# Lift, weights and fetches of a mixed head pair moved by one to two steps in an attention kernel on one core

## The chip, the cores and the metric

The kernel runs on one core of a Trainium2 chip. The metric is the device time of one execution in microseconds (us); of several runs the median is taken. Engines are named as in the profile: PE (TensorE), PEld (its weight load), DVE (VectorE), ACT (ScalarE), POOL (GpSimd), SP (SyncE, which only issues DMAs). ACT and POOL issue DMAs of their own besides their work.

## What is computed

One layer of a decoder trunk on 2048 tokens of width 1024, in float32: attention beside a pooling branch, a gated MLP with a short convolution, a gated embedding, and norms between them. Only the attention's last step matters here. A head's output is a mixture of branches, weighted by their softmax denominators:

```python
for window, dil in DIL_PATTERNS:                 # ((128, 1), (512, 4), (2048, 16))
    o, m, d = _dilated_branch(q, k, v, slopes, window, dil)   # output, row max, denominator
...
w = d * jnp.exp(m - jnp.max(m, axis=0, keepdims=True))
w = w / jnp.sum(w, axis=0, keepdims=True)
return jnp.sum(w[..., None] * o, axis=0)
```

The kernel computes two parts per head: a "near" one (window 128) and a "far" one (the two dilated patterns together). It keeps for each query the negated maximum and the denominator of both parts, and mixes at the end: `exp(lo - max)` with `lo` the smaller of the two negated maxima, a division by the weighted sum of denominators, and two products with the unnormalised outputs.

## The kernel before

The program has three phases: projection (to about 400 us of the profile), attention (to about 720 us), and the rest (out projection, MLP, gate). The attention phase, `phase_attention` (from L486), goes over 8 heads in 4 pairs. A head has 16 blocks of 128 queries, so there are 128 steps `s`, 32 to a pair. PE, ACT, DVE and POOL run in the order in which the code is written; that order is made by the loop over `s` (L739), which at each step calls a fixed list of stages (`CFG["ord"]`, L44), each for the step `s - lag`. In one step DVE does the near maximum (L577), the far maximum (L583), the low part of a split (L617) and often a sum of two halves (L660); ACT does two exponentials (L589, L593), a cast (L613) and a copy (L659); PE does scores (L561, L562, L572, L573), transposes (L600) and products with the values (L628, L642). `CFG["perm"]` turns the blocks so that the four steps of a group have far widths of 512, 384, 256 and 128.

SP loads the next head's queries, keys and biases (one load per step, in the first 8 steps of a head) and the next pair's values, as buffers come free.

The pairs 0, 1 and 2 are mixed while the next pair is being computed (the last pair is mixed in another way, in `last_near`, `last_far`, `last_weights`). The stage "M" (`mix`, L705) does it, by the number `d` of steps since the pair's end, so d = 0 is the first step of the next pair:

- d = 0: `mix_stats` (L761): PE transposes the pair's maxima and denominators, DVE copies them to `sx` and `sy`.
- d = 1: `mix_stats_store`: ACT issues two stores to DRAM, `std<-sx` (L776) and `stf<-sy` (L777).
- d = 4: `mix_stats_load`: ACT issues two loads in another order of axes, `sn<-std` (L784) and `sf<-stf` (L788). They wait for the stores, and what stands behind them on ACT waits too.
- d = `m[0]`: `mix_lift` (L858): three DVE operations of 128x32 (L862, L865, L866), the first of which reads `sn` and `sf`; then one exponential on ACT (L867, `wts<-ex`).
- d = `m[1]`: `mix_weights` (L870): five small DVE operations (L874 to L879), then POOL issues the store `wd<-wts` (L880).
- d = `m[2] + m[3] * c` for the four chunks c of 512 queries: `mix_fetch` (L885): POOL issues two loads `wb<-wd` (L891), each spread over 64 partitions.
- `m[4]` steps after its fetch: `mix_products` (L896): POOL multiplies and adds (L901, L902, L908, into the buffers m1 and m3).
- `m[5]` steps after its fetch: `mix_store` (L917): POOL splits the result (L913, L914) and issues two stores, `mh<-ah` and `ml<-al` (L924, L925).

```python
if d == CFG["m"][0]:
    mix_lift(nc, g, mx, pairs[pr])
if d == CFG["m"][1]:
    mix_weights(nc, g, mx, pr, pairs[pr])
for c in range(NCH):
    if d == CFG["m"][2] + CFG["m"][3] * c:
        mix_fetch(nc, g, mx, nc.gpsimd, pr, pairs[pr], c)
    if d == CFG["m"][2] + CFG["m"][3] * c + CFG["m"][4]:
        mix_products(nc, g, mx, nc.gpsimd, pairs[pr], c)
```

In the list of stages "M" stands ahead of the step's maxima, so the lift of d = 9 is on DVE between the low part (L617) of one step and the near maximum (L577) of the next. POOL has no other work in this phase. At the end of the phase `last_near` (L794) copies the last pair's statistics on DVE (L806) into buffers, one of which is the buffer m3 that POOL's products of pair 2 read last in L908.

Of the kernel before, what the change touches and what calls it, by code (L numbers as in the profile page):

```python
# [20 lines left out]
S = 2048  # L21
# [19 lines left out]
V_N = V_CB + 2 * NF  # L41


CFG = {"tt": 2, "ee": 2, 'ord': [['B', 0], ['M', 0], ['N', 0], ['S', 1], ['o', 7], ['F', 0], ['h', 2], ['nm', 0], ['p', 7], ['fm', 0], ['l', 2], ['T', 1], ['V', 6], ['W', 6], ['ne', 0], ['fe', 0]], 'perm': [3, 2, 1, 0], 'fp': [[0], [1], [2], [3]], 'np': [[0, -1], [1], [2], [3]], 'm': [9, 10, 13, 4, 6, 7]}  # L44


class Shared:
# [438 lines left out]
def phase_attention(tc, g, mx, near_b, far_b):  # L486
# [5 lines left out]
    with ExitStack() as ctx:  # L492
# [42 lines left out]
        def begin(s):  # L535
# [7 lines left out]
            st = steps[s] = Shared()  # L543
            st.n = n = n - n % 4 + CFG["perm"][n % 4]
            st.t, st.pt, st.e = heads[h], pairs[h // 2], h % 2
# [5 lines left out]
            st.d1, st.d3 = st.pt.st1[:, 1, st.e, n : n + 1], st.pt.st3[:, st.r, 1, st.e, st.i : st.i + 1]  # L551
            st.tt = sb.tile([P, 768], F32, tag="tt", bufs=CFG["tt"], name="tt")
            st.ee = sb.tile([P, 768], F32, tag="ee", bufs=CFG["ee"], name="ee")

# [64 lines left out]
        def near_pv(gi, kbs, first):  # L619
            gr, q0 = groups[gi], 4 * (gi % 4)  # L620
            for kb in kbs:
                if q0 + kb < 0:
                    continue
                m0, m1 = max(0, kb), min(3, kb + 1)
                b0, b1 = 4 * m0 + kb + 1, 4 * m1 + kb + 1
                kt = q0 + kb
                for pt in (gr.h, gr.l):
                    nc.tensor.matmul(  # L628
                        gr.o[:, m0 * P : (m1 + 1) * P],
                        vals[gi // 8, "v1", kt // 4][:, kt % 4, gi // 4 % 2, :],  # L630
                        pt[:, b0 : b1 + 1 : 4, :],
                        start=first,
                        stop=False,
                        skip_group_check=True,
                    )
                    first = False

        def far_pv(gi, kbs, first):
            gr = groups[gi]
            for kb in kbs:  # L640
                for pt in (gr.h, gr.l):
                    nc.tensor.matmul(  # L642
                        gr.o[:, kb * P :],
                        vals[gi // 8, "v3", gi % 4][:, kb, gi // 4 % 2, :],
                        pt[:, 6 * kb + 2 : 18 + kb : 5, :],
                        start=first,
                        stop=False,
                        skip_group_check=True,
                    )
                    first = False  # L650
# [11 lines left out]
        def values(v):  # L662
# [4 lines left out]
            if part < 2:  # L667
                far_pv(gi, CFG["fp"][2 * part], part == 0)
            else:
                near_pv(gi, CFG["np"][2 * part - 4], part == 2)  # L670

        def values_b(v):
            gi, part = v // 4, v % 4
            if part < 2:
                far_pv(gi, CFG["fp"][2 * part + 1], False)
            else:
# [1210 lines left out]
```

## Time and profile before

| what | value |
|---|---|
| median of 3 runs | 2520.25 us (2514.61, 2520.25, 2520.33) |
| the profiled execution | 2522.12 us, its span 2519.8 us |
| mean granted TensorE clock | 0.98 |
| busy: PE, DVE, ACT, POOL | 2407.5, 1588.8, 1108.6, 515.7 us |
| std store issued, pairs 0, 1, 2 | at 475.48, 551.84, 637.59 us |
| sf load issued, pairs 0, 1, 2 | at 484.64, 562.66, 646.01 us |
| L862 started, pairs 0, 1, 2 | at 498.30, 582.36, 665.04 us |

Rows of the timeline give the start, the duration, the engine, line and operation, output and inputs, and in brackets how long the engine had been idle before it and what ended that idle time. Rows of the waits give who waited for whom: total, times, longest. Rows of the chain of waits give the start and length of each piece of the chain that ended last. Rows of the stage table give a stretch, its length, the busy time of PE, PEld, DVE, ACT and POOL (with the number of instructions), the granted clock, the DMA share and GB/s.

### The profile page before, as it was taken

To read this page: it belongs to the slowest core of one execution; us is meant where nothing else is said; L and a number is where in the kernel's file an instruction comes from. 1 tells how busy PE (TensorE), PEld (TensorE's weight loads), DVE (VectorE), ACT (ScalarE), POOL (GpSimd) and SP (SyncE) were. 2 spreads that over 40 slices of the span, in tenths; PEclk is the share of its full clock that TensorE was granted. 3 is DMA by queue.
4 is the path that set the end of the run, shared out by engine and by line. 5 is a ranking of instruction groups with operands and counts; after the bars stand their busy time and mean duration, and the time that the engine had idled before them with its cause. 6 is when DMAs were issued, how large, how long until landed. Compare 5 with 4: busy or idle time off the path is not lost.

```text
span 2519.8 us, 31897 instructions
## 1 busy us (share of the span) xinstructions
PE 2407.5 (96%) x11515; PEld 2022.4 (80%) x11515; DVE 1588.8 (63%) x2416; ACT 1108.6 (44%) x1923; POOL 515.7 (20%) x423
## 2 busy tenths in 40 slices
PE   8999998888779999999999999999999999999998
PEld 7888887777767877888887888888788888887888
DVE  6635427777774467888888666666535374435755
ACT  5423326887751135544446444444323242323322
POOL 3312221053430023333340000000122222221000
PEclk9999999999879999999999999999999999999999
DMA  7534358687646674555556334333546464635332
GB/s 240 174 120 180 142 178 248 166 193 180 164 164 221 223 252 167 167 177 181 175 194 211 122 117 138 121 114 117 191 134 222 149 219 150 208 122 173 124 105 88
DMA packets 209052, 424.08 MB, mean 168 GB/s; under 512 B 42464, under 2 KB 68896, under 8 KB 205824
## 3 DMA queue, kind: packets, MB, share of 16 engines
q1 hardware_dynamic: 170576, 368.41, 46.4%
q0 software_dynamic: 18672, 25.88, 3.1%
q10 hardware_dynamic: 19648, 27.77, 3.1%
q8 instruction: 90, 1.47, 0.2%
q14 instruction: 66, 0.54, 0.1%
HBM read 290.01 MB, written 131.89 MB: 167 GB/s over the span
## 4 chain that ended last, share of the span: by engine, by line
PE 79%; DMA 6%; DVE 6%; issue 3%; ACT 2%; POOL 0%; SPq 0%; ACTq 0%; POOLq 0%; DVEq 0%
PE ua L1315 18%; PE uc L1315 9%; PE dn L90 6%; PE dn L91 6%; PE dn L89 6%; PE ub L1315 4%; PE z L91 4%; PE z L89 4%; PE z L90 4%; PE o L89 2%; PE o L91 2%; PE o L90 2%; PE gp L89 2%; PE gp L91 2%; PE gp L90 2%
## 5 line engine op out<-in xcount | busy, mean ns | idle before, releaser
L89 PE MATMUL dn<-ah,hd 128*128 128x512 f32 x704 | 275.3, 391 | 2.8 <-ACT ah L84 2.8
L90 PE MATMUL dn<-al,hd 128*128 128x512 f32 x704 | 274.9, 391 | 1.7 <-DVE al L85 1.7
L91 PE MATMUL dn<-ah,ld 128*128 128x512 f32 x704 | 274.6, 390 | 0.0
L85 POOL TENSOR_TENSOR ld<-rd,hd 128x1024 fp32r<-128x1024 f32 x42 | 100.9, 2403 | 812.8 <-ACT hd L84 812.8
L84 ACT CAST hd<-rd 128x1024 fp32r<-128x1024 f32 x88 | 92.5, 1052 | 266.3 <-PE dn L90 230.9
L85 DVE TENSOR_TENSOR al<-ra,ah 128x512 fp32r<-128x512 f32 x88 | 116.8, 1330 | 136.0 <-ACT ah L84 136.0
L89 PE MATMUL z<-hnh,wh 128*128 128x512 f32 (+1 forms) x480 | 170.3, 355 | 9.9 <-ACT hnh L252 5.8
L90 PE MATMUL z<-hnl,wh 128*128 128x512 f32 (+1 forms) x480 | 170.0, 354 | 2.7 <-DVE hnl L253 2.6
L91 PE MATMUL z<-hnh,wl 128*128 128x512 f32 (+1 forms) x480 | 169.9, 354 | 2.3 <-POOL wl L85 1.7
L89 PEld LDWEIGHTS dn<-ah,hd 128*128 128x128 f32 x704 | 132.7, 188 | 31.0 <-ACT ah L84 3.2
L90 PEld LDWEIGHTS dn<-al,hd 128*128 128x128 f32 x704 | 132.7, 188 | 29.8 <-DVE al L85 2.2
L91 PEld LDWEIGHTS dn<-ah,ld 128*128 128x128 f32 x704 | 132.7, 189 | 27.4
L85 DVE TENSOR_TENSOR wu<-ru,wu 128x1024 fp32r<-128x1024 f32 x88 | 127.4, 1448 | 0.0
L155 DVE TENSOR_TENSOR acc<-acc,sq 128x512 f32<-128x512 f32 (+1 forms) x125 | 90.2, 722 | 47.6 <-ACT sq L154 34.6
L1315 PE MATMUL uc<-a22h,wu 128*128 128x512 f32 x352 | 115.7, 389 | 1.8 <-DVE uv L1338 1.8
L1315 PE MATMUL ua<-s2h,wu 128*128 128x512 f32 x352 | 115.8, 390 | 1.1 <-ACT ug L1452 1.1
L1315 PE MATMUL uc<-s3h,wu 128*128 128x512 f32 x352 | 116.2, 390 | 0.3 <-ACT s3h L1371 0.3
L1315 PE MATMUL ub<-a12h,wu 128*128 128x512 f32 x352 | 115.9, 390 | 0.3 <-ACT a12h L1371 0.3
L1315 PE MATMUL ua<-s4h,wu 128*128 128x512 f32 x352 | 115.5, 389 | 0.0
L1315 PE MATMUL ua<-s1h,wu 128*128 128x512 f32 x352 | 115.5, 389 | 0.0
L1315 PE MATMUL ua<-a11h,wu 128*128 128x512 f32 x352 | 115.5, 389 | 0.0
L85 DVE TENSOR_TENSOR ld<-rd,hd 128x1024 fp32r<-128x1024 f32 x46 | 56.2, 1223 | 89.1 <-ACT hd L84 89.1
(317 smaller groups left out, 6474.4 us busy)
## 6 DMA issues: line engine op xcount, KB each, us to landing
rd<-in_w_down_dram SPq DMA_DIRECT2D x88, 512.0 KB, 3.6
ru<-in_w_up_dram SPq DMA_DIRECT2D x66, 512.0 KB, 4.1
ra<-act SPq DMA_DIRECT2D x88, 256.0 KB, 3.8
act<-yg SPq DMA_DIRECT2D x43, 512.0 KB, 3.1
wr<-in_w_in_dram SPq DMA_DIRECT2D x64, 256.0 KB, 4.0
nt<-h SPq DMA_DIRECT2D x56, 256.0 KB, 3.9
h<-h SPq DMA_DIRECT2D x56, 256.0 KB, 5.6
td<-t SPq DMA_DIRECT2D x22, 512.0 KB, 2.6
```

The lines of the kernel that those rows point to most:

```text
L84: nc.scalar.copy(hi, src)
L85: (low or nc.gpsimd).tensor_tensor(lo, src, fp(hi), op=ALU.subtract)
L89: nc.tensor.matmul(ps, wh, ah, start=first, stop=False)
L90: nc.tensor.matmul(ps, wh, al, start=False, stop=False)
L91: nc.tensor.matmul(ps, wl, ah, start=False, stop=last)
L155: nc.vector.tensor_tensor(acc[:, :n], acc[:, :n], sq[:, :n], op=ALU.add)
L1315: nc.tensor.matmul(pst, x[:, ksl], y, start=first and k == 0 and n == 0, stop=k == HK - 1 and n == 2, skip_group_check=True)
```

## The change

One line changes, the table `CFG` at L44, in its last entry `m`:

```diff
-'m': [9, 10, 13, 4, 6, 7]
+'m': [11, 12, 14, 4, 5, 6]
```

The lift is at d = 11 instead of 9 and the weights at d = 12 instead of 10. The fetches of the four chunks are at d = 14, 18, 22, 26 instead of 13, 17, 21, 25. The products come 5 steps behind their fetch instead of 6, that is, at 19, 23, 27, 31 in both kernels, and the stores at 20, 24, 28, 32 in both.

The instructions of PE and of SP stand in the same order in both kernels. POOL's do too: only the buffers' numbers differ, since its fetches, products and stores pass no other POOL instruction. On DVE and ACT the lift and the weights change places. This is the difference on DVE at pair 1's lift (the row of L862 is the lift's first operation; rows with ISA are the maxima, each with the row that reads its result; `ptl` is the low part, `s` the sum of halves):

```order
+L577 ISA tt,st_5565<-sn,nb_5117 128x256
+L577 ISA st_5565 128x1
+L583 ISA tt,st_5566<-sf,fb_5118 128x384
+L583 ISA st_5566 128x1
+L617 TENSOR_TENSOR ptl<-tp,pth 128x384
+L577 ISA tt,st_5565<-sn,nb_5117 128x256
+L577 ISA st_5565 128x1
+L660 TENSOR_TENSOR s_5567<-o,ev 64x512
+L583 ISA tt,st_5566<-sf,fb_5118 128x256
+L583 ISA st_5566 128x1
+L617 TENSOR_TENSOR ptl<-tp,pth 128x768
 L862 TENSOR_TENSOR lo<-sn,sf 128x32
```

The DVE work of two steps (far widths 384 and 256) now stands ahead of L862, the first reader of `sf`; in the rows of L577 and L583 `sn` and `sf` are score tiles of the same name in PSUM, not the loaded statistics. On ACT, at the same place, the exponential of the lift (L867) moves in the same way:

```order
 L593 ACTIVATE ee,st_5566<-tt,st_5566 128x512
+L613 CAST pth<-tp 128x384
+L589 ACTIVATE ee,st_5565<-tt,st_5565 128x256
+L593 ACTIVATE ee,st_5566<-tt,st_5566 128x384
+L659 COPY ev<-o 64x512
+L613 CAST pth<-tp 128x768
+L589 ACTIVATE ee,st_5565<-tt,st_5565 128x256
+L593 ACTIVATE ee,st_5566<-tt,st_5566 128x256
 L867 ACTIVATE wts<-ex 128x64
```

Seven ACT operations of the same two steps now stand ahead of L867. The pieces at pairs 0 and 2 are alike.

More of the change, by code (lines that the diff above doesn't have):

```diff
@@ L41 @@
 V_N = V_CB + 2 * NF
-CFG = {"tt": 2, "ee": 2, 'ord': [['B', 0], ['M', 0], ['N', 0], ['S', 1], ['o', 7], ['F', 0], ['h', 2], ['nm', 0], ['p', 7], ['fm', 0], ['l', 2], ['T', 1], ['V', 6], ['W', 6], ['ne', 0], ['fe', 0]], 'perm': [3, 2, 1, 0], 'fp': [[0], [1], [2], [3]], 'np': [[0, -1], [1], [2], [3]], 'm': [9, 10, 13, 4, 6, 7]}
+CFG = {"tt": 2, "ee": 2, 'ord': [['B', 0], ['M', 0], ['N', 0], ['S', 1], ['o', 7], ['F', 0], ['h', 2], ['nm', 0], ['p', 7], ['fm', 0], ['l', 2], ['T', 1], ['V', 6], ['W', 6], ['ne', 0], ['fe', 0]], 'perm': [3, 2, 1, 0], 'fp': [[0], [1], [2], [3]], 'np': [[0, -1], [1], [2], [3]], 'm': [11, 12, 14, 4, 5, 6]}
 class Shared:
```

## The prediction

> **What bounds the kernel now.** I read the page first, then the stage table, the waits, the chain and the timelines of the attention phase.
>
> ```profile
> PE 2407.5 (96%) x11515; PEld 2022.4 (80%) x11515; DVE 1588.8 (63%) x2416; ACT 1108.6 (44%) x1923; POOL 515.7 (20%) x423
> ```
>
> PE bounds the program as a whole. The change touches only the attention phase, and there the picture is another. The waits from 398 to 740 us:
>
> ```profile
> ACT wts L867 <- DVE ex L866: 13.7, 3, 7.2
> DVE lo L862 <- DMA sf<-stf: 12.9, 2, 6.9
> PE sn L572 <- DVE st L577: 13.6, 3, 6.4
> ```
>
> Twice DVE stands at the lift's first operation because the statistics `sf` haven't landed; ACT then stands at the lift's exponential, and PE runs out of work, since its next scores need the maximum (L577) queued behind the lift. The chain that ended last goes through these two loads:
>
> ```profile
> 562.66 19.68 DMA sf<-stf
> ...
> 646.01 18.94 DMA sf<-stf
> ```
>
> So these are not idle times of an engine off the path: the phase waits for them. DVE's timeline shows what they cost. I take the stretch from the L577 of step d = 8 to that of d = 13, which holds the lift and the weights, in all three pairs:
>
> ```profile
> 495.90 0.42 DVE L577 CUSTOM_DVE_ANT_0 tt<-sn,nb 128x256 f32<-128x256 f32 x1
> ...
> 505.09 0.42 DVE L577 CUSTOM_DVE_ANT_0 tt<-sn,nb 128x256 f32<-128x256 f32 x1
> ...
> 506.88 0.68 DVE L617 TENSOR_TENSOR ptl<-tp,pth 128x512 fp32r<-128x512 f32 x1
> 507.65 0.42 DVE L577 CUSTOM_DVE_ANT_0 tt<-sn,nb 128x256 f32<-128x256 f32 x1
> ...
> 509.54 0.42 DVE L577 CUSTOM_DVE_ANT_0 tt<-sn,nb 128x256 f32<-128x256 f32 x1 [0.32 <-PE sn L573]
> ...
> 510.13 0.68 DVE L660 TENSOR_TENSOR s<-o,ev 64x512 f32<-64x512 f32 x1 [0.16 <-ACT ev L659]
> ...
> 511.07 0.95 DVE L617 TENSOR_TENSOR ptl<-tp,pth 128x768 fp32r<-128x768 f32 x1
> ...
> 513.80 0.42 DVE L577 CUSTOM_DVE_ANT_0 tt<-sn,nb 128x256 f32<-128x256 f32 x1
> ```
>
> ```profile
> 572.90 0.42 DVE L577 CUSTOM_DVE_ANT_0 tt<-sn,nb 128x256 f32<-128x256 f32 x1
> ...
> 582.36 0.19 DVE L862 TENSOR_TENSOR lo<-sn,sf 128x32 f32<-128x32 f32 x1 [6.91 <-DMA sf<-stf]
> ...
> 593.39 0.42 DVE L577 CUSTOM_DVE_ANT_0 tt<-sn,nb 128x256 f32<-128x256 f32 x1
> ...
> 656.54 0.43 DVE L577 CUSTOM_DVE_ANT_0 tt<-sn,nb 128x256 f32<-128x256 f32 x1
> ...
> 665.04 0.19 DVE L862 TENSOR_TENSOR lo<-sn,sf 128x32 f32<-128x32 f32 x1 [5.95 <-DMA sf<-stf]
> ...
> 675.95 0.42 DVE L577 CUSTOM_DVE_ANT_0 tt<-sn,nb 128x256 f32<-128x256 f32 x1
> ```
>
> Pair 0, which doesn't wait, takes 507.65 - 495.90 = 11.75 us for these five steps. Pair 1 takes 593.39 - 572.90 = 20.49 us and pair 2 675.95 - 656.54 = 19.41 us. The late `sf` thus costs 8.74 and 7.66 us, 16.40 us in all. The marked waits are 12.86 us of this. The other 3.54 us (1.83 and 1.71) come behind them, when PE is slow:
>
> ```profile
> 583.27 0.58 PE L572 MATMUL sn<-ks,qhh 128*128 128x256 f32 x1 [6.42 <-DVE st L577]
> ```
>
> ```profile
> 586.00:589.00 3.00, 2.77 (x10) 2.58 (x11) 1.83 (x7) 1.73 (x6) 1.15 (x2) 0.50 0.09 16
> ...
> 650.00:652.00 2.00, 2.00 (x12) 2.00 (x11) 0.73 (x3) 1.16 (x5) 0.00 (x0) 0.50 1.14 296
> ```
>
> The granted clock is 0.50 behind the gap of 6.42 us on PE.
>
> **What is taken away: two steps less to wait.** The lift now has the DVE work of two more steps ahead of it. In pair 0 that work, at its ordinary pace, runs from the end of one L617 (506.88 + 0.68 = 507.56) to the end of the L617 two steps on (511.07 + 0.95 = 512.02): 4.46 us. Of that DVE idles 0.32 + 0.16 us, so 3.98 us is the least. I take 4.46 us, since the phase's pace is that of all engines together. The loads of `sn` and `sf` stay at d = 4 and SP's order doesn't change, so I let `sf` land when it does now. What remains of the waits is 6.91 - 4.46 = 2.45 us and 5.95 - 4.46 = 1.49 us (2.93 and 1.97 at most). Queued behind the shortened wait is what was queued behind the old one: the next maxima, and PE and ACT (at L867, `wts<-ex`) behind them.
>
> **The clock.** PE's gap was 0.49 us shorter than DVE's wait (6.42 for 6.91), so gaps of 1.96 and 1.00 us remain. The nearest row is a gap of 2.53 us earlier in pair 2:
>
> ```profile
> 647.93 0.39 PE L628 MATMUL o<-pth,v 128*128 128x256 f32 x1 [2.53 <-DVE s L660]
> ```
>
> Behind it the stretch 650 to 652 us, quoted above, has a clock of 0.50. So a gap of 1.96 us is near one that slowed PE, and 1.00 us is not. I take half of 1.83 us for pair 1 (0.9) and a tenth of 1.71 us for pair 2 (0.2), 1.1 us together, between 0 and 3.5. The Trainium skill ("TensorE: Matmul & The Clock Gate", Part 1: The HAM clock gate) has it that the clock halves only after an idle window of about 3.4 us. By that rule neither remaining gap would cost anything, and the sum below would be 1.1 us better; the trace's 2.53 us gap speaks against taking the rule so strictly here.
>
> **The eight operations in their new place.** In pair 0 the four steps with lift and weights take 505.09 - 495.90 = 9.19 us, four steps without them 513.80 - 505.09 = 8.71 us. So they cost 0.48 us where they are. The weights alone fill
>
> ```profile
> 500.01 0.18 DVE L874 TENSOR_TENSOR dn<-wts,sn 128x32 f32<-128x32 f32 x1
> ...
> 501.08 0.42 DVE L577 CUSTOM_DVE_ANT_0 tt<-sn,nb 128x256 f32<-128x256 f32 x1
> ```
>
> 1.07 us, and three lift operations of 0.19 us make 1.64 us at most: much of it fills waits like the 0.32 and 0.16 us above. In the new place they can cost from 0 to 1.64 us, a change between -0.48 and +1.16 per pair. The steps are of the same kind; I take +0.1, for three pairs +0.3 us.
>
> **What comes later: POOL's chain.** POOL does nothing else in this phase, and its instructions keep their order; moving the fetches by one step and setting products and stores one step nearer changes nothing on its queue. But its chain starts when the weights are ready (L880 waits for DVE). In pair 0 that is two steps later. In pairs 1 and 2 it is nearly the same moment as before, since the lift still waits for `sf` and then only one step of DVE work is between lift and weights as before. The next pair, however, ends earlier against that chain by what pair 1 gains (8.74 - 2.45 - 0.9 = 5.4 us), so POOL's last stores meet pair 2's statistics as pair 0's stores met pair 1's. What that is worth I read from the difference between the two:
>
> ```profile
> 563.07 0.58 ACT L659 COPY ev<-o 64x512 f32<-64x512 f32 x1 [4.51 <-DMA v<-vn]
> ```
>
> ```profile
> 646.57 0.58 ACT L659 COPY ev<-o 64x512 f32<-64x512 f32 x1 [2.25 <-DMA stf<-sy]
> ```
>
> ACT stands at the loads of d = 4, until the stores of d = 1 have landed, for 4.51 us in pair 1 and 2.25 us in pair 2 (the releaser's name differs, the place is the same), and `sf` takes 19.68 us against 18.94. If pair 2 becomes like pair 1 it loses 2.26 + 0.74 = 3.0 us. I take half, 1.5 us.
>
> **The sum.** 16.40 - 2.45 - 1.49 - 1.1 - 0.3 - 1.5 = 9.6 us saved. Everything behind the attention phase waits for its end and should shift with it. The profiled execution took 2522.12 us, 2.3 us over its span and 1.9 us over the median of 2520.25; I take the saving off the median: **2510.7 us**. With every term at its good end (no clock, no loss in pair 2, -0.48 three times) it is 13.9 us, 2506.4; with every term at its bad end 16.40 - 4.90 - 3.5 - 3.5 - 3.0 = 1.5 us, 2518.8. About 0.3% (7.6 us) is what a measurement of this kernel can tell from no change.
>
> **Rival A: `sf` lands later too, and the wait follows the lift.** The load's time hangs on what else moves. Rows of pair 0's window, then of pair 1's:
>
> ```profile
> sf<-stf ACTq DMA_DIRECT2D x1, 32.0 KB, 9.8
> ```
>
> ```profile
> DMA packets 3454, 4.57 MB, mean 218 GB/s; under 512 B 1234, under 2 KB 2961, under 8 KB 3216
> ...
> q0 software_dynamic: 163, 0.53, 8.1%
> ...
> sf<-stf ACTq DMA_DIRECT2D x1, 32.0 KB, 19.7
> ```
>
> 32 KB took 9.8 us in pair 0, where no mixing was under way, and 19.7 us in pair 1, with 0.53 MB of POOL's queue (q0) in the window: one chunk's two stores. If POOL's chain comes later and a second chunk's stores (0.53 MB at 218 GB/s, 2.4 us) fall into the window of both pairs, 2 x 2.4 = 4.8 us of the saving go: 2515.5 us. With two more chunks all 9.6 us go: 2520.3 us. For it: pair 0's chain starts two steps later. Against it: POOL stands for long stretches on its own loads, which can swallow a later start. The Trainium skill ("DMA: Bandwidth & Descriptors", Queues, rings and completion order) says that each DMA engine takes turns between the queues that have work; by that rule every further packet of POOL's queue makes the turns of `sf` longer, which is this rival's mechanism, and the two landing times agree with it.
>
> **Rival B, slower: the end of the phase waits for POOL.** `last_near` on DVE (L806) writes the buffer that POOL's L908 of pair 2's last chunk reads.
>
> ```profile
> 561.17 1.26 POOL L908 TENSOR_TENSOR m<-m,m 128x512 f32<-128x512 f32 x1
> ```
>
> ```profile
> 673.62 0.42 DVE L577 CUSTOM_DVE_ANT_0 tt<-sn,nb 128x256 f32<-128x256 f32 x1 [0.99 <-PE sn L573]
> ...
> 709.55 1.30 POOL L908 TENSOR_TENSOR m<-m,m 128x512 f32<-128x512 f32 x1
> ...
> 717.75 1.28 DVE L806 COPY nr<-tpn 8x512 f32<-8x512 f32 x2 [1.22 <-PE tpn L799]
> ```
>
> Pair 2's weights would end about where the L577 of d = 12 starts now, 673.62; from there L806 is 44.1 us away. POOL's chain from the end of the weights took 43 us in pair 2 (about 667.9 to 710.85), so 1 us is left. In pair 0 it took 561.17 + 1.26 - 501.08 = 61.4 us. If pair 2's becomes like that, L806 waits 17.3 us: 2510.7 + 17.3 = 2528.0 us. From a chain of 44.1 + 9.6 = 53.7 us on the kernel is slower than before. Against it: pair 2's chain has no next head's loads beside it, pair 0's had.
>
> **Rival C: the change removes the wait altogether.** `sf` lands earlier by what remains of the wait, because fewer of POOL's stores meet it, and PE's clock never falls: 16.40 - 0.3 = 16.1 us, 2504.2 us. Nothing that the change does makes this likely. That it does nothing at all is excluded, since the lift does move past two steps of DVE and ACT work.
>
> **How the numbers follow.** Forecast 0.60 (0.20 of it that PE's clock stays up through both gaps, 2510.7 - 1.1 = 2509.6 us, which is also what the Trainium skill's rule on the clock gate, cited above, would give), rival A 0.30, rival B 0.05, rival C 0.05. The range from 2506 to 2520 holds the forecast's own bounds and rival A, and leaves out B and C and a little of A. Faster by over 0.3% needs 7.6 us: most of the forecast (0.50), C (0.05) and a little of A (0.03), 0.58. Within 0.3%: the rest of the forecast, nearly all of A, and B's milder half, 0.39. Slower: 0.03.
>
> **What the profile after would show.** Right: the wait of L862 on `sf` is two of about 2.5 and 1.5 us; `sf` still takes 19 to 20 us; the stretch from the L577 of d = 8 to that of d = 13 falls from 20.5 and 19.4 us by 4 to 6 us each; the chain still passes through `sf`; PE's gaps there are about 2 and 1 us, with a clock of 0.50 behind the first at most. Wrong: `sf` taking over 22 us (rival A), a wait of L806 on POOL (B), or waits of the old size at another place, such as ACT's at d = 4 growing by more than 3 us.

## The result, and the profile after

| | before | after |
|---|---|---|
| median of 18 runs each | 2520.29 us (2509.34 to 2527.28) | 2528.99 us (2518.96 to 2532.0) |
| the profiled execution, its span | 2522.12, 2519.8 us | 2518.96, 2517.0 us |
| a second and a third profile of the changed kernel | | 2525.37 (span 2522.9) and 2529.57 (span 2527.5) us |

The ratio is 1.0032, with a 95% interval of 1.0019 to 1.0045: the changed kernel is slower by about 8 us, where 9.6 us of saving were forecast. The execution that was profiled with the result is the shortest of its 18, so it is not typical; two more profiles of the same kernel were taken (`e_aft2`, `e_aft3`, below). `e_aft3` is near the median, and "a typical execution" means it from here on.

The wait that the change was made for, that of the lift (L862) for `sf`, is smaller than forecast. This is what is left of it in the profile with the result; in both later profiles there is none at all (before: 12.9 us in two):

```profile
DVE lo L862 <- DMA sf<-stf: 0.3, 1, 0.3
```

But the typical execution has another, which the kernel before does not have (waits of 398 to 760 us):

```profile
DVE s L660 <- POOL m L902: 11.7, 2, 6.7
```

L660 is the sum of two halves, and L902 the second product of POOL's chain. They have nothing to do with each other but a buffer: `s3`, the far part of a pair's output, has two buffers. At about d = 8 of a boundary the first far sum of pair p + 2 is written into the buffer of pair p, and POOL must have read it for its last chunk by then. Here are both on DVE's timeline, with the lift that follows each:

```profile
582.75 0.68 DVE L660 TENSOR_TENSOR s<-o,ev 64x512 f32<-64x512 f32 x1 [4.97 <-POOL m L902]
...
590.53 0.17 DVE L862 TENSOR_TENSOR lo<-sn,sf 128x32 f32<-128x32 f32 x1
...
668.57 0.68 DVE L660 TENSOR_TENSOR s<-o,ev 64x512 f32<-64x512 f32 x1 [6.74 <-POOL m L902]
...
676.36 0.17 DVE L862 TENSOR_TENSOR lo<-sn,sf 128x32 f32<-128x32 f32 x1
```

The first is in pair 1's boundary (pair 2 writes when pair 0's last chunk is read), the second in pair 2's. In the kernel before, the same sum found the buffer long free:

```profile
573.56 0.68 DVE L660 TENSOR_TENSOR s<-o,ev 64x512 f32<-64x512 f32 x1 [0.22 <-ACT ev L659]
```

```profile
559.58 1.51 POOL L902 TENSOR_TENSOR m<-s,wb 128x512 f32<-128x512 f32 x1 [2.85 <-DMA wb<-wd]
```

L902 ended at 561.09, 12.5 us ahead of that sum. Behind the new wait PE stands as it stood behind the old one, and its clock falls in the same way (last but two column: the granted clock):

```profile
583.48 0.58 PE L628 MATMUL o<-pth,v 128*128 128x256 f32 x1 [5.27 <-DVE s L660]
...
669.30 0.58 PE L628 MATMUL o<-pth,v 128*128 128x256 f32 x1 [7.04 <-DVE s L660]
```

```profile
583.00:586.00 3.00, 2.52 (x11) 2.42 (x12) 2.26 (x7) 1.49 (x4) 2.86 (x3) 0.50 0.70 157
...
669.00:672.00 3.00, 2.69 (x11) 2.60 (x12) 2.26 (x7) 1.66 (x5) 2.86 (x4) 0.50 0.36 87
```

The chain of waits of that execution, which went through `sf` before, now goes through POOL:

```profile
553.76 27.38 DMA wb<-wd
581.13 0.07 issue
581.20 1.52 POOL m L902
...
639.11 27.84 DMA wb<-wd
667.02 1.52 POOL m L902
668.57 0.69 DVE s L660
669.30 1.23 PE o L628 x4
```

Where the time went is seen in the stretches that hold the boundaries, from the L577 of d = 4 to that of d = 16 (starts on DVE's timeline). Twelve steps elsewhere in the phase take about 27 us (45.1 us for 20).

| d = 4 to 16 of | pair 0 | pair 1 | pair 2 | sum |
|---|---|---|---|---|
| before | 31.26 | 40.66 | 37.46 | 109.38 |
| after, shortest execution | 31.27 | 36.78 | 35.44 | 103.49 |
| after, second profile | 31.74 | 43.59 | 35.95 | 111.28 |
| after, typical | 33.51 | 40.05 | 41.86 | 115.42 |

By this table the shortest execution is 5.9 us shorter than the profile of before, and the typical one 6.0 us longer. Each row is one execution. The profile of `e_bown` (below), whose lift stands where it did before and whose time is that of the kernel before, has a sum of 102.95 us, so a difference of some 6 us between two rows isn't by itself the work of the change.

### The profile page after: what moved, and what is told of

It reads as the page before. It is cut to its first block, busy times and chain, and to the rows that moved or that the text cites. A ratio compares the mean times of both kernels' runs of the same rounds, so it can differ in the third digit from the quotient of the medians.

```text
span 2517.0 us, 31897 instructions
## 1 busy us (share of the span) xinstructions
PE 2406.0 (96%) x11515; PEld 2022.0 (80%) x11515; DVE 1592.4 (63%) x2416; ACT 1108.8 (44%) x1923; POOL 515.3 (20%) x423
## 4 chain that ended last, share of the span: by engine, by line
PE 74%; issue 8%; DMA 8%; DVE 4%; POOL 2%; ACT 1%; SPq 0%; POOLq 0%; DVEq 0%; ACTq 0%
PE ua L1315 18%; PE uc L1315 9%; PE dn L90 6%; PE dn L89 6%; PE dn L91 6%; PE ub L1315 4%; DMA wb<-wd 4%; PE z L91 4%; PE z L89 4%; PE z L90 4%; PE o L89 2%; PE o L91 2%; PE o L90 2%; PE gp L89 2%; PE gp L91 2%
```

## Why POOL is late

POOL's chain for pair 0, the kernel before first (weights stored, chunk 0's first loads, its product, chunk 3's loads), then the typical execution after:

```profile
502.03 0.77 POOL L880 DMA_DIRECT2D wd<-wts  x1 [100.30 <-DVE st L577]
504.49 2.43 POOL L891 DMA_DIRECT2D wb<-wd  x3 [1.70 <-DMA wd<-wts]
...
514.99 1.58 POOL L902 TENSOR_TENSOR m<-s,wb 128x512 f32<-128x512 f32 x1
...
543.93 1.65 POOL L891 DMA_DIRECT2D wb<-wd  x2
```

```profile
509.50 0.77 POOL L880 DMA_DIRECT2D wd<-wts  x1 [108.07 <-DVE st L577]
511.96 2.43 POOL L891 DMA_DIRECT2D wb<-wd  x3 [1.70 <-DMA wd<-wts]
...
531.77 1.57 POOL L902 TENSOR_TENSOR m<-s,wb 128x512 f32<-128x512 f32 x1 [7.80 <-DMA wb<-wd]
...
552.95 1.65 POOL L891 DMA_DIRECT2D wb<-wd  x2
...
581.20 1.51 POOL L902 TENSOR_TENSOR m<-s,wb 128x512 f32<-128x512 f32 x1 [6.73 <-DMA wb<-wd]
```

The weights are 7.5 us later, but chunk 0's product 16.8 us and chunk 3's product 581.20 - 559.58 = 21.6 us. The delay grows where the loads run beside others. SP starts the next head's loads at 512.40 us before and at 515.63 after, so 3.2 of the 7.5 us are that this whole boundary runs later in the typical execution, and 4.2 us are the two steps:

```profile
512.40 0.45 SPq L56 DMA_DIRECT2D qhh<-qh  x1
```

```profile
515.63 0.45 SPq L56 DMA_DIRECT2D qhh<-qh  x1
```

Before, POOL's first three loads were issued 7.9 us ahead of them, after, 3.7 us. The medians from issue to landing (last column, us), for the loads issued in 503 to 510 us of before and in 510 to 517 us of after:

```profile
wb<-wd POOLq DMA_DIRECT2D x3, 256.0 KB, 9.3
```

```profile
wb<-wd POOLq DMA_DIRECT2D x3, 256.0 KB, 18.9
```

Other profiles with all loads and four steps between the chunks agree. With 7.7 to 7.9 us between POOL's first load and SP's, chunk 0's second product starts 10.0 to 11.4 us after that load was issued (`before`, `e_bown`, `e_bnw3`, `e_bs3`, `e_p2only`). With 4.8 us it starts 13.6 and 16.3 us after it (`after`, `e_own`), and with 3.4 to 3.7 us 18.4 to 22.0 us (`e_aft2`, `e_aft3`, `e_same`, `e_pair2`, `e_wlate`, `e_nw3`, `e_s3`).

And chunk 3's two loads, issued 9 us later, fall among the loads of the next pair's queries and values; before, then after:

```profile
wb<-wd POOLq DMA_DIRECT2D x2, 256.0 KB, 13.1
```

```profile
wb<-wd POOLq DMA_DIRECT2D x2, 256.0 KB, 23.8
```

## The theories

**Theory 3** (the two buffers): weights that are two steps later start POOL's chain later, the loads of the next head stretch it, and L660 waits for L902. Since the next pair's statistics then meet POOL's last loads and stores, `sf` lands later too, so the wait at the lift comes back when the wait of L660 is taken away ("the wait follows"). **Theory 1** (the tail, rival B of the prediction): L806 waits for POOL's L908 at the end of the phase. **Theory 2** (the loads of the statistics): ACT's wait at d = 4 or the landing of `sf` alone makes the loss. A rival to the buffer's part of Theory 3 is that POOL's traffic beside the loads does it all. Ratios are to the kernel before, from runs on the same chip, with the 95% interval.

## The experiments

**`e_aft2`, `e_aft3`: the changed kernel again.** No edit.

> The changed kernel once more, unchanged, for a second profile, since the one shown with the result is of the shortest of its executions. Theory 3 with the wait that follows the lift: one or two waits of L660 on POOL's L902, 5 to 11 us each, and a span of 2522 to 2530 us. If the loss isn't there: no such wait, and waits of L862 on sf of 5 us or more, or of L806 on POOL.

> The same as the run ahead of it, a third profile of the changed kernel: one or two waits of L660 on L902 of 5 to 11 us each, a span of 2522 to 2530 us.

Measured: 2525.37 and 2529.57 us. The first has one wait of L660 (this row), the second the two shown above, and neither has a wait of L862:

```profile
DVE s L660 <- POOL m L902: 9.6, 1, 9.6
```

In the shortest execution, which has no such wait, L902 of pair 0 ended 7.0 us ahead of the sum (569.72 against 576.74). Whether a given execution waits is a matter of some us in POOL's loads.

**`e_same`: lift and weights late, the rest of the table as before.**

```diff
-'m': [11, 12, 14, 4, 5, 6]
+'m': [11, 12, 13, 4, 6, 7]
```

> Same instructions as the changed kernel (the fetches stand at d = 13 again, products and stores where they were; POOL's order doesn't depend on it): about 2528 us, ratio to before 1.003. It is run for its profile, since the changed kernel's profiled execution (2518.96 us) was the shortest of its 18. Theory 1 (the tail): POOL's chain of pair 2 ends late, and L806 waits for L908 by 8 us or more where the first profile had 0.28. Theory 2 (the loads): the stretch from d = 0 to d = 13 of pairs 1 and 2 is longer than in the first profile by 8 us or more in sum, in the wait at ACT's loads of d = 4 or at L862, and L806 waits under 2 us.

Measured: 2525.54 us, ratio 1.0026 [1.0011, 1.0042].

```profile
DVE s L660 <- POOL m L902: 9.2, 1, 9.2
```

The slot of the fetches and the distance to the products are not the cause; every engine's instructions stand as in the changed kernel. The wait of L660 was first seen here.

**`e_own`, `e_bown`: the tail's buffer.** The changed kernel and the kernel before, with a buffer of its own for the copy of L806, so that it can't wait for L908:

```diff
-sb.tile([P, CH], F32, tag="m3", bufs=1, name="nr")[:8]
+sb.tile([P, CH], F32, tag="nr2", bufs=1, name="nr")[:8]
```

> The changed kernel, with a buffer of its own for the copy of the last pair's statistics (L806), so that it doesn't wait for POOL's L908. Theory 1: ratio to before 0.996 to 1.000 (about 2510 to 2519 us). Theory 2: 1.003 as the changed kernel, since nothing is changed at the loads.

> The kernel before with that buffer of its own. Theory 1: as before within 0.1%, since POOL is 7 us ahead of L806 there. Theory 2: the same.

Measured: 2522.2 us, 1.0010 [0.9994, 1.0027], and 2519.25 us, 1.0002 [0.9987, 1.0017]. The first lies between the two expectations, nearer to the tail theory's, but its profile still shows a wait of L660 of 5.8 us, and the longest wait of L806 on POOL in any profile is 0.28 us, in the shortest execution of the changed kernel:

```profile
713.18 0.68 DVE L806 COPY nr<-tpn 8x512 f32<-8x512 f32 x1 [0.28 <-POOL m L908]
```

The interval touches that of the changed kernel, so this pair alone decides nothing.

**`e_pair2`, `e_p2only`: which pair.** The changed kernel with pair 2's lift and weights where they were, and the other way round:

```diff
-if d == CFG["m"][0]:
+if d == (9 if pr == 2 else 11):
...
-if d == CFG["m"][1]:
+if d == (10 if pr == 2 else 12):
```

```diff
-if d == CFG["m"][0]:
+if d == (9 if pr < 2 else 11):
...
-if d == CFG["m"][1]:
+if d == (10 if pr < 2 else 12):
```

> Lift and weights at d = 11 and 12 for pairs 0 and 1, at 9 and 10 as before for pair 2. Theory 1: POOL's last chain starts in time again, ratio 0.996 to 1.000. Theory 2: half of the loss stays, 1.001 to 1.002, as pair 1 still has it; L806 doesn't wait in either.

> Lift and weights later (d = 11 and 12) for pair 2 alone, pairs 0 and 1 as before (9 and 10). Theory 3: no pair writes over pair 2's s3, so its chain may be late; pairs 0 and 1 start in time: no wait of L660 on POOL, pair 2's wait for its statistics shrinks by about 4.5 us: ratio 0.997 to 0.999. Theory 2: a third to a half of the loss, 1.001 to 1.002. Theory 1 (L806 waits for POOL): 1.002 to 1.003, with a wait of L806 of some us.

Measured: 2528.63 us, 1.0031 [1.0015, 1.0047], and 2520.37 us, 0.9997 [0.9984, 1.0009]. All of the loss is there when only pairs 0 and 1 are late, and none when only pair 2 is. The tail comes behind pair 2 alone, so Theory 1 falls. The small gain that Theory 3 expected of `e_p2only` (0.997 to 0.999) is not seen either. Pairs 0 and 1 are those whose `s3` buffers pairs 2 and 3 write again:

```profile
DVE s L660 <- POOL m L902: 17.1, 2, 10.8
```

**`e_wlate`: only the weights late.** The lift goes back to d = 9; the weights stay at 12.

```diff
-'m': [11, 12, 14, 4, 5, 6]
+'m': [9, 12, 14, 4, 5, 6]
```

> The lift as before (d = 9), the weights two steps later (12 instead of 10): nothing is moved away from the late load, only POOL's chain starts later. Theory 3: the loss is POOL's late start, so ratio 1.002 to 1.004, with waits of L660 on L902 of 6 us or more. Theory 2: as before within 0.1%, since the loads and the lift stand where they stood.

Measured: 2533.59 us, 1.0047 [1.0029, 1.0064], from six runs; the middle of it is a little above what Theory 3 expected, and the interval leaves out Theory 2.

```profile
DVE s L660 <- POOL m L902: 17.2, 2, 8.8
DVE lo L862 <- DMA sf<-stf: 5.1, 2, 3.0
```

So the late weights bring the loss without the late lift.

**`e_nw3`, `e_bnw3`: the last product without its wait for the load.** Chunk 3 of pairs 0 to 2 is multiplied by the weights of chunk 2, so its right result is left out; its own loads are issued but not read. After, then before with the same edit:

```diff
-pt.__dict__.setdefault("wb", {})[c] = wb
+pt.held = pt.held if c == NCH - 1 else wb; pt.__dict__.setdefault("wb", {})[c] = pt.held
```

> The changed kernel, but the products of a pair's last chunk (pairs 0 to 2) multiply by the weights of the chunk ahead of it; the last chunk's fetch is still issued and lands, and nobody reads it. So that part of the output is left out, the traffic stays, and only POOL's wait for that landing is gone. Theory 3 (two buffers): with the later weights POOL reads s3 for the last chunk so late that DVE's first half sum (L660) of the pair after the next, which writes the same buffer, waits for it: without POOL's wait, no wait of L660 on L902 is left, and the ratio to before is 0.994 to 0.998 (2505 to 2515 us). Theory 2 (later loads of the statistics, ACT's wait at d = 4): ratio 1.002 to 1.004 as the changed kernel.

> The kernel before with the same edit (the last chunk's products take the weights of the chunk ahead; the fetch stays and is not read). Theory 3: within 0.2% of before, since L902 ends 12 us ahead of L660 there. Theory 2: within 0.2% of before.

Measured: 2523.23 us, 1.0009 [0.9998, 1.0021], and 2521.11 us, 0.9993 [0.9982, 1.0004]. The wait of L660 is gone and with it a good part of the loss (half of it, 1.0009 / 0.9993 = 1.0016, against the kernel before with the same edit). But the gain that Theory 3 expected here (0.994 to 0.998) does not appear: the lift of the changed kernel waits again, and as long as in the kernel before with the same edit, though it stands two steps later. After, then before:

```profile
DVE lo L862 <- DMA sf<-stf: 7.7, 2, 6.2
```

```profile
DVE lo L862 <- DMA sf<-stf: 7.6, 2, 6.6
```

**`e_s3`, `e_bs3`: a third buffer.** Nothing is left out here: `s3` gets three buffers, and to make room `ah` and `al` get two and `ev` one, in the kernel after and in the kernel before.

```diff
-pt.s3 = mx.tile([P, 4, CH], F32, tag="s3", bufs=2, name="s3")
+pt.s3 = mx.tile([P, 4, CH], F32, tag="s3", bufs=3, name="s3")
...
-ev = sb.tile([P, CH], F32, tag="ev", bufs=2, name="ev")
+ev = sb.tile([P, CH], F32, tag="ev", bufs=1, name="ev")
...
-hi = sb.tile([P, CH], F32R, tag="ah", bufs=3, name="ah")
-lo = sb.tile([P, CH], F32R, tag="al", bufs=3, name="al")
+hi = sb.tile([P, CH], F32R, tag="ah", bufs=2, name="ah")
+lo = sb.tile([P, CH], F32R, tag="al", bufs=2, name="al")
```

> The changed kernel with three buffers s3 instead of two, so that the half sum L660 of pair 2 (or 3) no longer has to wait until POOL's product L902 of the last chunk of pair 0 (or 1) has read its buffer. To make room, ah and al have two buffers instead of three and ev one instead of two; all instructions and transfers stay. Theory 3 (the loss is this wait and nothing else): no wait of L660 on L902, and since the change then keeps what it saves, a ratio of 0.995 to 0.999. Theory 3 with the wait that follows the lift (statistics land later beside POOL's later chain): no wait of L660, one or two waits of L862 on sf of 1 to 6 us, ratio 1.000 to 1.002. Rival (the loss is POOL's traffic beside the loads alone): ratio 1.003 as without the third buffer. Whatever the smaller ah, al and ev cost shows in the kernel before with the same three sizes.

> The kernel before with the same three sizes (three s3, two ah and al, one ev). It has no wait of L660 on L902 in its profile, so a third s3 brings nothing; the smaller buffers may cost a little, since ACT's copy L659 then needs the half sum ahead to be done. All theories: ratio 1.000 to 1.002.

Measured: 2522.93 us, 1.0004 [0.9994, 1.0015], and 2518.44 us, 0.9993 [0.9979, 1.0006]. With all transfers in place the loss of 0.32% is down to 0.04%. Against the kernel before with the same sizes it is 1.0004 / 0.9993 = 1.0011, a third of it; by the two medians it is 4.5 us, about half of the 8.7. So the wait for the buffer is a half to two thirds of the loss as measured here, and roughly so, since each ratio's interval reaches 0.1% to either side; the traffic beside the loads is not all. The gain of the forecast does not appear even then. In pair 1 the lift waits, and `sf` takes 24.7 us (window 540 to 600 us; the second fence is `e_s3`, the third `e_bs3`). In pair 2 it doesn't wait, but ACT has stood 7.49 us at the loads of d = 4 instead, where it stood under 2 us in `e_bs3`:

```profile
DVE lo L862 <- DMA sf<-stf: 6.6, 1, 6.6
```

```profile
sf<-stf ACTq DMA_DIRECT2D x1, 32.0 KB, 24.7
```

```profile
sf<-stf ACTq DMA_DIRECT2D x1, 32.0 KB, 20.0
```

**`e_nf3`, `e_bnf3`: without the last chunk's loads.** As `e_nw3` and `e_bnw3` (the same part of the result is left out), but chunk 3's two loads are not issued at all:

```diff
-wb = []
-for a in range(2):
+wb = pt.held if c == NCH - 1 else []
+for a in range(0 if c == NCH - 1 else 2):
...
-pt.__dict__.setdefault("wb", {})[c] = wb
+pt.__dict__.setdefault("wb", {})[c] = pt.held = wb
```

> The changed kernel without the fetch of the last chunk's weights: the last chunk of pairs 0, 1 and 2 is multiplied by the weights of the chunk ahead of it, and its two loads of 256 KB are left out, so its result is another. This takes away both the late end of the last product and a quarter of POOL's loads. Theory 3 with the wait that follows the lift: no wait of L660 on L902; fewer of POOL's packets beside the loads of the next head; sf still meets the stores of the chunk ahead, so L862 may still wait up to 6 us; ratio 0.996 to 1.001. If the wait of L660 alone made the loss and the fetch itself costs nothing: the ratio of the kernel that issues the fetch and leaves it unread, 1.001. Rival (POOL's traffic beside the loads): 0.995 to 0.998.

> The kernel before without the fetch of the last chunk's weights (the same part of the result is another). If POOL's loads at the boundary delay the statistics of the next pair: sf in less than 19 us, shorter waits of L862 and a ratio of 0.996 to 0.999. If they don't: 0.999 to 1.000, as with the fetch left unread.

Measured: 2509.56 us, 0.9953 [0.9938, 0.9968], and 2510.14 us, 0.9956 [0.994, 0.9973]. Two loads of 256 KB per boundary, for which only POOL waits in the kernel before, cost it about 10 us in three pairs; with the same loads issued and not read (`e_bnw3`) it was no faster. `e_nf3` is where the rival of Theory 3 expected it (0.995 to 0.998), but the kernel before gains as much, so this cost is not what the change added: without these loads the change is worth nothing either way (0.9953 / 0.9956 = 0.9997, from six runs each). `sf` in pair 1's window of `e_bnf3`, and all that is left of the lift's wait there:

```profile
sf<-stf ACTq DMA_DIRECT2D x1, 32.0 KB, 13.8
```

```profile
DVE lo L862 <- DMA sf<-stf: 0.8, 1, 0.8
```

One landing proves little here: in `e_bown`, with these loads, `sf` took 13.8 us in pair 1 as well.

**`e_sp3`, `e_asp3`: POOL's chain asked to end sooner.** Nothing is left out; the chunks come every three steps instead of four, in the kernel before and after (in the kernel before this also puts the fetches of chunks 2 and 3 on POOL ahead of the split and stores of chunks 0 and 1).

```diff
-'m': [9, 10, 13, 4, 6, 7]
+'m': [9, 10, 13, 3, 6, 7]
```

```diff
-'m': [11, 12, 14, 4, 5, 6]
+'m': [11, 12, 14, 3, 5, 6]
```

> The kernel before with three steps instead of four between the chunks: fetches at 13, 16, 19, 22, products at 19, 22, 25, 28, stores at 20, 23, 26, 29. Nothing is left out; POOL's chain is asked to end three steps (about 7 us) earlier. If POOL's loads at the pair's boundary are what delays the statistics: less of q0 in the 20 us behind the pair's end, sf in less than 19 us, ratio 0.995 to 0.998. If POOL is bound by its loads and not by the steps, its chain ends when it did: 0.999 to 1.001.

> The changed kernel with three steps instead of four between the chunks (fetches at 14, 17, 20, 23, products at 19, 22, 25, 28, stores at 20, 23, 26, 29). If the late end of POOL's chain makes the loss: L902 of pair 0's last chunk ends some us earlier, no wait or a short one of L660, and a ratio of 0.996 to 1.000. If the chain is bound by its loads: as the changed kernel, 1.002 to 1.004.

Measured: 2518.01 us, 0.9992 [0.9984, 1.0001], and 2525.38 us, 1.0017 [1.0006, 1.0027]. In `e_sp3` the product of chunk 3 of pair 0 starts at 555.35 us, 4.2 us sooner where 7 were asked for, and the ratio is what was expected of a chain that is bound by its loads. In `e_asp3` it starts at 575.76 us, still too late; the ratio lies between the two expectations, its interval overlaps that of the changed kernel, and L660 still waits:

```profile
DVE s L660 <- POOL m L902: 10.5, 2, 6.4
```

No version that does all the work is faster than the kernel before by more than the measurement can tell.

## Why the prediction was wrong, point by point

Two steps failed. The first turned a gain into a loss, the second took the gain away.

- **The step on POOL's chain**: that the moved fetches and products change "nothing on its queue", with L806 at the end of the phase as the one reader of a late chain. The order of POOL's instructions is unchanged, but not when they run, and L660 was not named as a waiter though it reuses `s3` every second pair. In the trace of before it has 12.5 us to spare in pair 1. In the typical execution the chain ends 21.6 us later and the sum itself is due 4.2 us later, so it waits 5.0 us. The prediction had the delay of the weights right (two steps) and treated it as if it stayed two steps. It does not: loads issued 4.2 us nearer to SP's take 18.9 instead of 9.3 us.
- **"In pairs 1 and 2 it is nearly the same moment as before"** failed with it: in pair 1 the chain starts at 594.28 us in the typical execution (L880 on POOL's timeline) and at 585.69 before, 8.6 us later. In the shortest execution, without the wait of L660, it held (586.95).
- **"I let `sf` land when it does now"** is the other step that failed, and rival A was right that it lands later. In pair 1 `sf` took 13.8 to 20.1 us, with a median of 19.7, in the five profiles in which pair 0's weights stand at d = 10 and all loads are issued (`before`, `e_bown`, `e_bnw3`, `e_bs3`, `e_p2only`). In the nine in which they stand at d = 12 (`after`, `e_aft2`, `e_aft3`, `e_same`, `e_own`, `e_pair2`, `e_wlate`, `e_nw3`, `e_s3`) it took 17.9 to 26.7 us, with a median of 24.0. That is 4.3 us more, about what two steps hide. In pair 2 the two groups don't differ so (medians of 18.7 and 19.5 us); where `sf` was quick there (9.1 to 13.3 us) ACT had stood 6.3 to 9.2 us at d = 4, so the time had only changed its place. Rival A gave at most no gain (2520.3 us), for it had no price for the buffer. The Trainium skill ("DMA: Bandwidth & Descriptors", Queues, rings and completion order) has the DMA engines take turns between queues; the later landings beside POOL's later loads and stores fit that, but no run counted the turns, and the two groups overlap.
- **The 16.40 us to be saved** were read from one execution. Over pair 0's time the stretches from d = 8 to d = 13 of pairs 1 and 2 cost 0.2 us in `e_bown`, 9.3 in `e_bnw3` and 16.2 in `e_bs3`, which have the lift where it was and the time of the kernel before (ratios 1.0002, 0.9993, 0.9993). So the cost changes by as much as its whole size from one execution to another, and the forecast took it at its upper end.
- **Two steps hide 4.46 us of the wait.** That can't be seen by itself: L862 no longer waits at all in the two later profiles, since L660 holds DVE ahead of it while `sf` lands. The 12.86 us of waiting are replaced by 9.6 and 11.7 us at another instruction. An estimate from the rows of `e_aft3`: without the waits of 4.97 and 6.74 us the lifts would be due at 585.6 and 669.6 us, and `sf` landed at 588.7 and 673.6 (issued at 567.02 and 650.03, with 21.7 and 23.6 us), so they would wait 3.2 and 4.0 us. By this the buffer's own price in that execution is 11.7 - 7.2 = 4.5 us, near what `e_s3` gives.
- **The clock.** 1.1 us were left for it. The gaps did not shrink: 5.27 and 7.04 us on PE, with a granted clock of 0.50 behind both. The old cost of 3.54 us stayed: the stretches from d = 8 to d = 13 take 18.71 and 20.93 us in the typical execution, and less the two waits and pair 0's 12.20 that leaves 1.5 and 2.0 us.
- **The eight operations' new place** was given +0.1 us per pair. In pair 0, which has neither wait, the stretch from d = 8 to d = 13 takes 12.41, 12.17 and 12.20 us in the three profiles after and 11.75 before: +0.4 to +0.7 us, inside the stated bounds. The +2.25 us of the typical execution in the table stand ahead of that: ACT waited 5.45 us at the loads of d = 4, and 2.87 before.
- **Pair 2's boundary as pair 1's (1.5 us)**: in pair 2 ACT stood 7.04, 6.29 and 3.56 us at d = 4 in the three profiles after and 2.25 before, so more, as the term has it. But profiles with the lift where it was scatter as far (9.24 us in `e_bown`, under 2 in `e_bs3`), so the runs neither show this term nor exclude it. `e_wlate` shows only that Theory 2 alone doesn't make the loss.
- **Rival B** named the right kind of cost (a late POOL chain meets a buffer that another engine needs) at the wrong place: at the tail the wait is 0.28 us or none.

In sum: two things hold the boundary, the late statistics and POOL's late chain. The change moved the lift away from the first and pushed the second past its slack. About a half to two thirds of the loss is the wait for the buffer (`e_s3`, `e_nw3`, the estimate above), and the forecast's gain is missing because the statistics come later as well and because the wait to be saved was read from an execution in which it was long. What stays open is how the rest divides between the landing of `sf` and ACT's wait at d = 4, and how much of POOL's stretching is the DMA engines' sharing and how much the time in which POOL itself stands at an issue.

## What to carry to other kernels

When a producer is moved later, follow every buffer that its consumers release, two rounds on as well as the next one, and write the slack of each beside the delay; an unchanged instruction order says nothing about that. Don't carry a delay through a chain of loads at its face value: look what the loads will run beside at the new time. And where two causes end a wait at nearly the same moment, expect that removing one shows the other; taking out a transfer that may stand behind both (here the last chunk's fetch, 0.45%) tells what it costs in all. A wait that one profile shows is worth reading in a second profile of the same kernel before it is put into a sum.

## What was not expected of the hardware

A load of 256 KB that POOL issues, spread over 64 partitions, takes 9.3 us before SP's loads start, 18.9 us when it starts 3.7 us ahead of them, and 27 to 28 us at a pair's boundary (27.38 and 27.84 in the chain above). The load of 32 KB on ACT's queue (`sf`) took from 9.3 to 15.7 us at pair 0's end, where no mixing is under way, in the profiles looked at, and from 9.1 (pair 2 of `e_bown`) to 26.7 us (pair 1 of `e_pair2`) at the others. One profile of one execution is a weak ground for such a time: a tenth of a per cent of this kernel is 2.5 us, less than that load varies from one execution to the next.
